# Logits of a sliding-window attention layer: 64 queries of two heads times 192 keys in place of 128 queries of one head times 256 keys

## Chip, core and metric

The kernel runs on one core of a Trainium2 chip. The metric is the time of one execution in microseconds of device time, the median of several runs. The core has five engines with queues of their own: TensorE (PE in the rows; its weight loads are listed apart as PEld), VectorE (DVE), ScalarE (ACT), GpSimd (POOL) and SyncE (SP), which here only issues DMAs.

## What is computed

The input is a sequence of 1024 tokens of width 1024. A first layer is a gated DeltaNet; after it, keys and values are computed once and shared. The second layer, which the change touches, is a sliding-window attention with 32 query heads of width 64 that share 4 key heads. Queries come in blocks of 128; a query sees itself and the 127 tokens before it, so of the 256 keys of two neighbouring blocks each query needs 128.

```python
def swa_sink_mixer(h, w_in, q_gain, sinks, w_out, k_band, v_band, bias, mask):
    q, z = jnp.split(h @ w_in, 2, axis=-1)
    q = rms_norm(q.reshape(B, T, B_Q_HEADS, B_HD), q_gain) * (B_HD ** -0.5)
    q = q.reshape(B, nb, BLOCK, B_KV_HEADS, B_GROUP, B_HD)
    logits = jnp.einsum("bnqkgd,bnskd->bnkgqs", q, k_band).astype(jnp.float32) + bias
    logits = jnp.where(mask[None, :, None, None], logits, -jnp.inf)
    sink = sinks.astype(jnp.float32).reshape(B_KV_HEADS, B_GROUP)[..., None, None]
    m = jnp.maximum(jnp.max(logits, axis=-1, keepdims=True), sink)
    p = jnp.exp(logits - m)
    probs = p / (jnp.sum(p, axis=-1, keepdims=True) + jnp.exp(sink - m))
    o = jnp.einsum("bnkgqs,bnskd->bnqkgd", probs.astype(v_band.dtype), v_band)
    o = o.reshape(B, T, B_W) * jax.nn.silu(z)
    return o @ w_out
```

## The kernel before

The heads of the second layer are worked on in 8 groups of 4 heads, each group in 8 blocks of 128 queries: 64 blocks, in the order of the list `blocks` in `b_attend`. Numbers are held as pairs of a rounded part and a rest, so a logit is the sum of two matmuls: the stationary operand is the block's queries (`qT`, which holds the rounded part of a head's queries above its rest), the moving operand the group's keys, once rounded (`kh`) and once the rest (`kl`).

The attention is one generator, `b_attend`, and the projections still to come (the next groups' queries, `b_q`, and the gate, `b_z`) are others; `interleave` draws from both by turns. TensorE's instructions stand exactly in the order in which the program is written (`manual_schedule`); the other engines' are put in order by the compiler's scheduler. Each step of the loop in `b_attend` turns the probabilities of block i, turns the queries of block i + 3, makes the logits of block i + 2 and the output of block i - 1, with matmuls of a projection between these.

In `logits`, for two heads at a time, a PSUM tile `lg` (two buffers) takes 256 columns of keys for each head: the block before, then the block itself. Since each query needs just 128 of them, VectorE folds them: where a key of the own block lies above the diagonal, `copy_predicated` (L1136) writes the logit of the previous block over it, by a mask of 128 x 128 (`self.up`). In the first block (n = 0) only the own block's 128 keys are computed and the masked ones get -1e30. Then a fused operation (L1140) adds the bias and takes the maximum with the sink, ScalarE takes the exponential (L1150), GpSimd multiplies by the reciprocal of the sum (L1154). In `turn`, TensorE transposes the folded probabilities, and the folding is undone there: the part for the own block is the transposed tile times a triangle (L1168, VectorE), that for the previous block is the rest (a copy on ScalarE, then a select on GpSimd, L1165). `values` multiplies both by the values.

The bias is loaded for each group from a table in HBM (`b_bias`, L1045), one group ahead. The sinks are loaded once in `b_consts` (L914), before the key gains `kg`. All weights come on the SP queue (L130); a weight of the second layer is scaled on GpSimd (L136) and split into a rounded part (`whi`) and a rest (`wlo`). The reciprocal root that normalises the queries (`rsqrt`, L111 to L119) is a chain of small operations on VectorE. `mm` is the PSUM tile of the projections (L939 to L941, L161 to L165), `pv` that of the output, `tp` that of the transposes.

Of the kernel before, what the change touches and what calls it, by code (L numbers as in the profile page):

```python
# [7 lines left out]
F32 = mybir.dt.float32  # L8
# [56 lines left out]
class Kernel:  # L65
# [837 lines left out]
    def b_consts(self, st):  # L903
# [190 lines left out]
    def b_attend(self, groups):  # L1094
# [15 lines left out]
        def q_turn(i):  # L1110
            t = qh.pop(i)
            ps = aps.tile([P, 4, P], F32R, name="tp", bufs=3)
            for e in range(4):
                nc.tensor.transpose(out=ps[:, e, :], in_=t[:, e, :, :].rearrange("p a d -> p (a d)"),
                                    identity=self.identr)
            qT[i] = bp.tile([P, 4, P], F32R, name="qT")
            nc.scalar.copy(out=qT[i], in_=self.f32(ps))

        def logits(i):

            X, n = blocks[i]
            kh, kl = X.keys
            sk = self.sink[:, 4 * X.hg:4 * X.hg + 4]
            q = qT.pop(i)
            k0 = 0 if n else P
            ksl = slice((n - 1) * P + k0, (n + 1) * P)
            L = Ls[i] = bp.tile([P, 4, P], F32, name="lsb", bufs=3)
            m = sb.tile([P, 4], F32, name="m")
            two = [P, 2, P]
            for pr in range(2):  # L1130
                ps = aps.tile([P, 2, 256], F32, name="lg")
                for j in range(2):
                    e = 2 * pr + j
                    nc.tensor.matmul(ps[:, j, k0:256], q[:, e, :], kh[:, ksl], start=True, stop=False)
                    nc.tensor.matmul(ps[:, j, k0:256], q[:, e, :], kl[:, ksl], start=False, stop=True)
                nc.vector.copy_predicated(ps[:, :, P:256], self.up.bitcast(I32).unsqueeze(1).broadcast_to(two),  # L1136
                                          ps[:, :, 0:P] if n else self.neg.unsqueeze(2).broadcast_to(two))
                for j in range(2):
                    e = 2 * pr + j
                    nc.vector.tensor_tensor_reduce(out=L[:, e, :], in0=ps[:, j, P:256], in1=X.bias[:, e, :],  # L1140
                                                   scale=1.0, scalar=sk[:, e:e + 1], op0=ALU.add, op1=ALU.max,
                                                   accum_out=m[:, e:e + 1])
# [3 lines left out]
            nc.vector.tensor_tensor(out=se, in0=sk, in1=m, op=ALU.subtract)  # L1146
            nc.scalar.activation(out=se, in_=se, func=AF.Exp)
# [8 lines left out]
        def turn(i):  # L1156
            L = Ls.pop(i)
            ps = aps.tile([P, 4, P], F32, name="tp", bufs=3)
            for e in range(4):
                nc.tensor.transpose(out=ps[:, e, :], in_=L[:, e, :], identity=self.ident)  # L1160
            pTs[i] = {}
            if blocks[i][1]:
                pT = pTs[i][0] = bp.tile([P, 4, P], F32, name="pT0")
                nc.scalar.copy(out=pT, in_=ps)
                nc.gpsimd.affine_select(out=pT, in_=pT, pattern=[[0, 4], [-1, P]], compare_op=ALU.is_gt, fill=0.0,  # L1165
                                        base=0, channel_multiplier=1)
            pT = pTs[i][1] = bp.tile([P, 4, P], F32, name="pT1")
            nc.vector.tensor_tensor(out=pT, in0=ps,  # L1168
                                    in1=self.cst[:, C_TRI:C_TRI + P].unsqueeze(1).broadcast_to([P, 4, P]), op=ALU.mult)

        def values(i):
            X, n = blocks[i]
            g, c = X.hg // 2, n % 4
            if c == 0:
                X.ot.append(bp.tile([P, 2, 512], F32, name="ot", bufs=4))
            po = aps.tile([P, 2, P], F32, name="pv", bufs=1)
# [6 lines left out]
            nc.scalar.copy(out=X.ot[-1][:, :, c * P:c * P + P], in_=po)  # L1183
            if n == NB - 1:
# [185 lines left out]
```

## Time and profile before

| | us |
|---|---|
| median of 3 runs | 1911.1 |
| lowest and highest run | 1909.24, 1915.82 |
| the profiled execution, its own time | 1906.83 |
| the profiled execution, span from first to last instruction | 1905.1 |

The profile is that of one execution, with start and duration of each instruction, what each engine waited for, and the granted clock of TensorE (0.994 of full speed over the span). All stretches are counted from the start of the span. The first layer, its output projection and the shared keys and values come first; the logits matmuls of the attention begin at 1174.5 us and end at 1698.4, with projections between them; from 1705 us to the end there is little but the last output projection.

### The profile page before, as it was taken

The numbers are of one execution on the slowest core, as the hardware profiler recorded it, in microseconds if no ns is written. First come the engines' busy times: TensorE is split into PE (matmuls) and PEld (weight loads), VectorE is DVE, ScalarE is ACT, GpSimd is POOL, SyncE is SP. The second block draws the span as 40 slices with busy tenths as digits, with TensorE's granted clock in tenths as the row PEclk, the third lists the DMA queues.
The fourth block names the chain that finished last, engine by engine and source line by source line (L and its number), as shares of the span: only waits on it lengthen the run. The fifth ranks groups of instructions, "written<-read, shape, count | busy, mean of one in ns | idle before, by whom it ended". The sixth has DMA issues, their size and how long they took to land.

```text
span 1905.1 us, 33635 instructions
## 1 busy us (share of the span) xinstructions
PE 1828.6 (96%) x13186; PEld 1562.9 (82%) x13186; DVE 1229.2 (65%) x2860; ACT 807.5 (42%) x1939; POOL 536.5 (28%) x554
## 2 busy tenths in 40 slices
PE   5999999999999999989999999999999999999999
PEld 4677778787877777767999998888788788879999
DVE  6767776858596776775545266777776776753432
ACT  4545353534435252433112043557756666771100
POOL 2222332323222222221311232333433343322111
PEclk9999999999999999999999999999999999999999
DMA  4511111112011211121655321111201111225542
GB/s 148 122 56 34 56 45 53 37 34 67 23 57 34 65 36 56 45 67 51 238 165 168 111 89 45 40 35 51 67 29 51 56 40 51 73 72 194 190 168 81
DMA packets 150115, 147.62 MB, mean 77 GB/s; under 512 B 7114, under 2 KB 124356, under 8 KB 149956
## 3 DMA queue, kind: packets, MB, share of 16 engines
q1 hardware_dynamic: 139616, 128.30, 21.4%
q10 hardware_dynamic: 10340, 17.16, 2.9%
q8 instruction: 104, 1.70, 0.4%
q14 instruction: 55, 0.45, 0.1%
HBM read 115.00 MB, written 30.44 MB: 76 GB/s over the span
## 4 chain that ended last, share of the span: by engine, by line
PE 36%; DVE 8%; ACT 3%; POOL 3%; issue 2%; DMA 1%; POOLq 0%; SPq 0%; ACTq 0%; DVEq 0%
PE acc L887 6%; PE acc L889 6%; PE acc L888 6%; PE mm L939 3%; PE mm L940 3%; PE mm L941 3%; PE pv L1181 2%; ACT lsb L1150 1%; PE mm L165 1%; PE mm L163 1%; PE mm L161 1%; DVE lsb L1140 1%; DVE wlo L138 1%; POOL lsb L1154 1%; PE tp L1160 1%
## 5 line engine op out<-in xcount | busy, mean ns | idle before, releaser
L161 PE MATMUL mm<-hh,whi 128*128 128x512 f32 (+1 forms) x1040 | 427.1, 411 | 1.8 <-ACT hh L223 1.7
L163 PE MATMUL mm<-hl,whi 128*128 128x512 f32 (+1 forms) x1040 | 417.5, 401 | 1.0 <-DVE hl L224 0.7
L165 PE MATMUL mm<-hh,wlo 128*128 128x512 f32 (+1 forms) x1040 | 414.8, 399 | 0.0
L138 DVE TENSOR_TENSOR wlo<-wraw,whi 128x1024 fp32r<-128x1024 f32 x141 | 178.7, 1268 | 241.0 <-POOL whi L134 216.0
L134 POOL TENSOR_SCALAR whi<-wraw 128x1024 fp32r<-128x1024 f32 x112 | 122.8, 1097 | 476.3 <-PE acc L889 241.4
L161 PEld LDWEIGHTS mm<-hh,whi 128*128 128x128 f32 x1040 | 197.0, 189 | 36.9 <-issue 5.2
L165 PEld LDWEIGHTS mm<-hh,wlo 128*128 128x128 f32 x1040 | 196.7, 189 | 36.5 <-issue 4.2
L163 PEld LDWEIGHTS mm<-hl,whi 128*128 128x128 f32 x1040 | 197.2, 190 | 34.1 <-issue 4.2
L939 PE MATMUL mm<-whi,hh 128*128 128x256 f32 x608 | 180.5, 297 | 0.0
L463 DVE SCALAR_TENSOR_TENSOR acc<-u,cw,acc 128x512 f32<-128x512 f32 x192 | 162.7, 849 | 26.5 <-POOL acc L460 24.3
L940 PE MATMUL mm<-wlo,hh 128*128 128x256 f32 x608 | 172.2, 283 | 0.0
L941 PE MATMUL mm<-whi,hl 128*128 128x256 f32 x608 | 172.2, 283 | 0.0
L887 PE MATMUL acc<-whi,hh 128*128 128x256 f32 x512 | 145.0, 283 | 0.0
L889 PE MATMUL acc<-whi,hl 128*128 128x256 f32 x512 | 144.9, 283 | 0.0
L888 PE MATMUL acc<-wlo,hh 128*128 128x256 f32 x512 | 144.9, 283 | 0.0
L1150 ACT ACTIVATE lsb<-lsb,nm 128x128 f32<-128x128 f32 x256 | 99.8, 392 | 64.1 <-DVE se L1146 54.6
L939 PEld LDWEIGHTS mm<-whi,hh 128*128 128x128 f32 x608 | 116.0, 191 | 11.0 <-issue 10.8
L940 PEld LDWEIGHTS mm<-wlo,hh 128*128 128x128 f32 x608 | 116.3, 191 | 0.2
L941 PEld LDWEIGHTS mm<-whi,hl 128*128 128x128 f32 x608 | 116.0, 191 | 0.0
L460 POOL TENSOR_SCALAR acc<-u,cw 128x512 f32<-128x512 f32 x64 | 63.9, 998 | 183.8 <-ACT u L456 169.6
L1154 POOL TENSOR_TENSOR lsb<-lsb,den 128x512 f32<-128x512 f32 x64 | 68.5, 1070 | 152.6 <-DVE den L1153 51.9
L887 PE MATMUL acc<-whi,oh 128*128 128x256 f32 x384 | 108.5, 283 | 0.0
(351 smaller groups left out, 4287.2 us busy)
## 6 DMA issues: line engine op xcount, KB each, us to landing
wraw<-in_a_w_in SPq DMA_DIRECT2D x48, 512.0 KB, 3.9
wraw<-in_a_w_out SPq DMA_DIRECT2D x32, 512.0 KB, 3.9
wraw<-in_b_w_in SPq DMA_DIRECT2D x32, 512.0 KB, 4.0
wraw<-in_b_w_out SPq DMA_DIRECT2D x32, 512.0 KB, 4.1
og<-zs SPq DMA_DIRECT2D x32, 256.0 KB, 2.0
ogT<-zs SPq DMA_DIRECT2D x28, 256.0 KB, 2.1
btab<-lt SPq DMA_DIRECT2D x1, 4096.0 KB
dm<-gd SPq DMA_DIRECT2D x8, 512.0 KB, 3.7
```

Source lines behind the costliest of these rows:

```text
L134: nc.gpsimd.tensor_scalar(out=hi, in0=raw, scalar1=1.0, scalar2=1.0, op0=ALU.mult, op1=ALU.mult)
L138: (nc.gpsimd if self.wcount < 3 else nc.vector).tensor_tensor(out=lo, in0=raw, in1=self.f32(hi), op=ALU.subtract)
L161: nc.tensor.matmul(ps, hi[:, k, :], hh[:, k, :], start=(k == 0), stop=False)
L163: nc.tensor.matmul(ps, hi[:, k, :], hl[:, k, :], start=False, stop=False)
L165: nc.tensor.matmul(ps, lo[:, k, :], hh[:, k, :], start=False, stop=(k == KT - 1))
L463: nc.vector.scalar_tensor_tensor(out=acc, in0=u[:, t:t + 512], scalar=cw[:, t, blk:blk + 1], in1=acc, op0=ALU.mult, op1=ALU.add)
L887: nc.tensor.matmul(po, oh[:, kk, ts], hi[:, kk, :], start=(k4 + kk + b == 0), stop=False)
L888: nc.tensor.matmul(po, oh[:, kk, ts], lo[:, kk, :], start=False, stop=False)
L889: nc.tensor.matmul(po, ol[:, kk, ts], hi[:, kk, :], start=False, stop=(k4 + kk + b == 7))
L939: nc.tensor.matmul(ps, hh[:, k, ts], hi[:, k % 4, :], start=(k == 0), stop=False)
L940: nc.tensor.matmul(ps, hh[:, k, ts], lo[:, k % 4, :], start=False, stop=False)
L941: nc.tensor.matmul(ps, hl[:, k, ts], hi[:, k % 4, :], start=False, stop=(k == KT - 1))
```

## The change

The 128 queries of a block are taken as two halves of 64. The halves of two heads stand together on the partitions (partition 64 e + t is query t of the half of head 2 j + e), so a stationary operand still has 128 columns. The moving operand is the 192 keys that a half can see: for the first half the previous block and the first 64 of the own, for the second the last 64 of the previous block and the own. Every query of the half sees the middle 64 of them; the first and the last 64 are seen in complementary triangles and are folded onto each other, by a mask of 64 columns (`le` for the first half, `gt` for the second). The tile index f = 2 hf + j now counts half and pair of heads in place of heads, in the logits, the probabilities, the bias, and the turned tiles; the sinks are laid out by partition halves. `turn` and `values` are rewritten to the new layout with views of runs of 64.

```diff
@@ b_consts
-        self.sink = sink = cp.tile([P, 32], F32, name="sink")
-        nc.sync.dma_start(sink, self.bcast_rows(I["b_sinks"], 32))
+        self.sink = sink = cp.tile([P, 16], F32, name="sink")
+        sk = I["b_sinks"]
+        for e in range(2):
+            nc.sync.dma_start(sink[64 * e:64 * e + 64, :],
+                              bass.AP(tensor=sk.tensor, offset=sk.offset + e, ap=[[0, 64], [2, 16], [1, 1]]))
@@ layer_b
-        self.up = self.cst[:, C_UP:C_UP + P]
+        above = self.cst[:, C_UP:C_UP + P]
+        self.gt, self.le = (bp.tile([P, 64], F32, name=i, bufs=1) for i in ("gt", "le"))
+        for r in (0, 64):
+            nc.vector.tensor_copy(self.gt[r:r + 64, :], above[r:r + 64, r:r + 64])
+        nc.vector.tensor_scalar(out=self.le, in0=self.gt, scalar1=-1.0, scalar2=1.0, op0=ALU.mult, op1=ALU.add)
@@ b_bias
-        self.nc.sync.dma_start(X.bias, bass.AP(tensor=tb.tensor, offset=tb.offset + 4 * X.hg * P * 256 + 127,
-                                               ap=[[255, P], [P * 256, 4], [1, P]]))
+        for e in range(2):
+            for hf in range(2):
+                self.nc.sync.dma_start(X.bias[64 * e:64 * e + 64, 2 * hf:2 * hf + 2, :],
+                                       bass.AP(tensor=tb.tensor,
+                                               offset=tb.offset + (4 * X.hg + e) * P * 256 + 64 * hf * 255 + 127,
+                                               ap=[[255, 64], [2 * P * 256, 2], [1, P]]))
@@ b_attend, q_turn
-            qT[i] = bp.tile([P, 4, P], F32R, name="qT")
-            nc.scalar.copy(out=qT[i], in_=self.f32(ps))
+            qT[i] = bp.tile([P, 2, 4, 64], F32R, name="qT")
+            nc.scalar.copy(out=qT[i].rearrange("p h e t -> p e h t"),
+                           in_=self.f32(ps).rearrange("p e (h t) -> p e h t", h=2))
@@ b_attend, logits
-            for pr in range(2):
+            for hf in range(2):
                 ps = aps.tile([P, 2, 256], F32, name="lg")
+                o = 64 * hf
+                cols = slice(0, 192) if n else slice(o, o + P)
+                ks = slice((n - 1) * P + o, (n - 1) * P + o + 192) if n else slice(0, P)
                 for j in range(2):
-                    e = 2 * pr + j
-                    nc.tensor.matmul(ps[:, j, k0:256], q[:, e, :], kh[:, ksl], start=True, stop=False)
-                    nc.tensor.matmul(ps[:, j, k0:256], q[:, e, :], kl[:, ksl], start=False, stop=True)
-                nc.vector.copy_predicated(ps[:, :, P:256], self.up.bitcast(I32).unsqueeze(1).broadcast_to(two),
-                                          ps[:, :, 0:P] if n else self.neg.unsqueeze(2).broadcast_to(two))
+                    w = q[:, hf, 2 * j:2 * j + 2, :].rearrange("p e t -> p (e t)")
+                    nc.tensor.matmul(ps[:, j, cols], w, kh[:, ks], start=True, stop=False)
+                    nc.tensor.matmul(ps[:, j, cols], w, kl[:, ks], start=False, stop=True)
+                if hf:
+                    nc.vector.copy_predicated(ps[:, :, P:192], gt, ps[:, :, 0:64] if n else neg)
+                elif n:
+                    nc.vector.copy_predicated(ps[:, :, 0:64], le, ps[:, :, P:192])
+                else:
+                    nc.vector.copy_predicated(ps[:, :, 0:64], gt, neg)
+                    nc.vector.memset(ps[:, :, 64:P], NEG)
...
@@ b_attend, turn
-                nc.gpsimd.affine_select(out=pT, in_=pT, pattern=[[0, 4], [-1, P]], compare_op=ALU.is_gt, fill=0.0,
-                                        base=0, channel_multiplier=1)
+                pv = pT.rearrange("p (h j) (e t) -> p h (j e) t", h=2, e=2)
+                nc.gpsimd.affine_select(out=pv, in_=pv, pattern=[[-64, 2], [0, 4], [-1, 64]], compare_op=ALU.is_gt,
+                                        fill=0.0, base=0, channel_multiplier=1)
...
@@ b_attend, values
-                    nc.tensor.matmul(po[e * 64:e * 64 + 64, :, :], v, pT[kb][:, e::2, :],
+                    nc.tensor.matmul(po[e * 64:e * 64 + 64, :, :], v, pT[kb][:, :, 64 * e:64 * e + 64],
                                      start=(kb == 1), stop=(kb == min(pT)))
```

TensorE's instructions stand in the same order as before, one for one; only the form of the logits matmuls differs. These are its rows from the last projection matmuls ahead of the second block's logits (n = 1), before:

```order
L939 MATMUL mm<-whi,hh_82 128x256
L940 MATMUL mm<-wlo,hh_82 128x256
L941 MATMUL mm<-whi,hl_83 128x256
L1134 MATMUL lg<-kh,qT 128x256
L1135 MATMUL lg<-kl,qT 128x256
```

And now:

```order
L943 MATMUL mm<-whi,hh_82 128x256
L944 MATMUL mm<-wlo,hh_82 128x256
L945 MATMUL mm<-whi,hl_83 128x256
L1151 MATMUL lg<-kh,qT 128x192
L1152 MATMUL lg<-kl,qT 128x192
```

What moved is only the shape, 192 columns for 256, and with it the line numbers.

On VectorE the scheduler sets the order anew. This is its order at the first block's logits (n = 0), where the reciprocal root of the next queries (L111 to L119, tiles `rqby` and `rqbt`) is drawn in between; before:

```order
L1136 COPY_PREDICATED lg<-cst,neg 128x2x128
L1068 TENSOR_SCALAR ssqb<-ssqb 128x16
L1107 TENSOR_TENSOR qh<-qr,qh 128x4x64
L111 TENSOR_SCALAR rqby<-ssqb 128x16
L1140 ISA lsb,m<-lg,bias,sink 128x128
L1140 ISA m 128x1
L113 TENSOR_SCALAR rqby<-rqby 128x16
L115 TENSOR_SCALAR ssqb<-ssqb 128x16
L1140 ISA lsb,m<-lg,bias,sink 128x128
L1140 ISA m 128x1
L117 TENSOR_TENSOR rqbt<-ssqb,rqby 128x16
L1136 COPY_PREDICATED lg<-cst,neg 128x2x128
```

And now:

```order
L1158 COPY_PREDICATED lg<-gt,neg 128x2x64
L1080 TENSOR_SCALAR ssqb<-ssqb 128x16
L1119 TENSOR_TENSOR qh<-qr,qh 128x4x64
L111 TENSOR_SCALAR rqby<-ssqb 128x16
L1159 MEMSET lg 128x2x64
L113 TENSOR_SCALAR rqby<-rqby 128x16
L115 TENSOR_SCALAR ssqb<-ssqb 128x16
L1162 ISA lsb,m<-lg,bias,sink 128x128
L1162 ISA m 128x1
L117 TENSOR_TENSOR rqbt<-ssqb,rqby 128x16
L1162 ISA lsb,m<-lg,bias,sink 128x128
L1162 ISA m 128x1
```

A fill (MEMSET) has come in, and the step L117 of the reciprocal root now stands between the two reductions (ISA) that read the first `lg` buffer, where it stood behind both.

## Rows read from the trace of the kernel before

**Rows 1.** Page, part 1: busy us of each engine, share of the span, instructions.
```profile
PE 1828.6 (96%) x13186; PEld 1562.9 (82%) x13186; DVE 1229.2 (65%) x2860; ACT 807.5 (42%) x1939; POOL 536.5 (28%) x554
```
**Rows 2.** Stretches: us; busy PE, PEld, DVE, ACT, POOL; granted clock; DMA share; GB/s.
```profile
1165.00:1710.00 545.00, 533.34 (x3672) 448.67 (x3671) 393.03 (x1372) 349.60 (x944) 187.29 (x211) 0.99 0.16 50
```
**Rows 3.** Waits of PE, 1165 to 1905 us: total us, times, longest.
```profile
PE tp L1160 <- POOL lsb L1154: 6.0, 4, 2.6
PE lg L1134 <- DVE m L1140: 5.0, 3, 4.2
```
**Rows 4.** Timeline of PE, a block with n = 1: start us, duration us, instruction.
```profile
1247.80 0.28 PE L1134 MATMUL lg<-kh,qT 128*128 128x256 f32 x1
1247.91 0.28 PE L1135 MATMUL lg<-kl,qT 128*128 128x256 f32 x1
...
1248.75 0.28 PE L939 MATMUL mm<-whi,hh 128*128 128x256 f32 x1
```
**Rows 5.** Timeline of PE, a block with n = 0.
```profile
1239.18 0.22 PE L1134 MATMUL lg<-kh,qT 128*128 128x128 f32 x1
1239.24 0.28 PE L1135 MATMUL lg<-kl,qT 128*128 128x128 f32 x1
1239.35 0.27 PE L1134 MATMUL lg<-kh,qT 128*128 128x128 f32 x1
1239.46 0.27 PE L1135 MATMUL lg<-kl,qT 128*128 128x128 f32 x1
...
1240.02 0.34 PE L939 MATMUL mm<-whi,hh 128*128 128x256 f32 x1
```
**Rows 6.** Timeline of PE's weight loads, the same block.
```profile
1239.19 0.19 PEld L1135 LDWEIGHTS lg<-kl,qT 128*128 128x128 f32 x1
1239.29 0.19 PEld L1134 LDWEIGHTS lg<-kh,qT 128*128 128x128 f32 x1
1239.40 0.19 PEld L1135 LDWEIGHTS lg<-kl,qT 128*128 128x128 f32 x1
```
**Rows 7.** Groups of weight loads by form: count, busy us, mean ns, idle before.
```profile
L1134 PEld LDWEIGHTS lg<-kh,qT 128*128 128x128 f32 x256 | 48.7, 190 | 8.0 <-DVE m L1140 4.4 <-issue 1.6 <-PE lg L1135 0.6
L341 PEld LDWEIGHTS mm<-hh,wab 128*32 128x32 f32 x16 | 1.7, 108 | 1.9 <-ACT u L456 0.4
```
**Rows 8.** Groups of DVE and POOL by form, 1165 to 1710 us.
```profile
L1140 DVE CUSTOM_DVE_ANT_0 lsb<-lg,bias,sink 128x128 f32<-128x128 f32 x256 | 77.9, 344 | 0.5
L1136 DVE COPY_PREDICATED lg<-cst,lg 128x256 f32<-128x256 int32 x112 | 44.6, 420 | 6.5 <-PE lg L1135 5.7
L1165 POOL TENSOR_SCALAR_AFFINE_SELECT pT<-pT 128x512 f32<-128x512 f32 x55 | 37.2, 677 | 82.2 <-ACT pT L1164 82.2
L1136 DVE COPY_PREDICATED_SCALAR lg<-cst,neg 128x256 f32 x16 | 7.6, 475 | 0.0
```
**Rows 9.** DMAs (KB each, us to landing), and issue and first use of `kg`.
```profile
abw<-in_a_w_in ACTq DMA_DIRECT2D x1, 64.0 KB, 4.2
bias<-btab SPq DMA_DIRECT2D x8, 256.0 KB, 2.9
L916 SPq DMA_DIRECT2D kg<-in_k_gain x1: 430/430/430, 17.7 to 17.7; - x1
L919 DVE SCALAR_TENSOR_TENSOR kg<-kg,lt x1: 218/218/218, 32.5 to 32.5; 128x64 f32<-128x64 f32 x1
```
**Rows 10.** Timeline of all engines at the start of the attention.
```profile
1177.57 1.90 POOL L136 TENSOR_TENSOR wraw<-wraw,gcolb 128x1024 f32<-128x1024 f32 x1 [1.09 <-DVE ssqb L115]
1177.62 1.87 DVE L117 TENSOR_TENSOR rqbt<-ssqb,rqby 128x16 f32<-128x16 f32 x1
...
1180.22 1.87 DVE L119 SCALAR_TENSOR_TENSOR rqby<-rqbt,rqby 128x16 f32<-128x16 f32 x1
...
1182.78 0.58 PE L1134 MATMUL lg<-kh,qT 128*128 128x256 f32 x1 [4.23 <-DVE m L1140]
```
**Rows 11.** Stretch with low clock, columns as in rows 2.
```profile
1180.00:1186.70 6.70, 3.92 (x19) 3.92 (x20) 6.61 (x28) 2.21 (x10) 2.31 (x2) 0.50 0.00 0
```

More of the change, by code (lines that the diff above doesn't have):

```diff
@@ L1122, in logits @@
             kh, kl = X.keys
-            sk = self.sink[:, 4 * X.hg:4 * X.hg + 4]
+            sk = self.sink[:, 2 * X.hg:2 * X.hg + 2]
             q = qT.pop(i)
-            k0 = 0 if n else P
-            ksl = slice((n - 1) * P + k0, (n + 1) * P)
             L = Ls[i] = bp.tile([P, 4, P], F32, name="lsb", bufs=3)
             m = sb.tile([P, 4], F32, name="m")
-            two = [P, 2, P]
-            for pr in range(2):
+            two = [P, 2, 64]
+            gt, le = (t.bitcast(I32).unsqueeze(1).broadcast_to(two) for t in (self.gt, self.le))
@@ L1131, in logits @@
+            neg = self.neg.unsqueeze(2).broadcast_to(two)
+            for hf in range(2):
                 ps = aps.tile([P, 2, 256], F32, name="lg")
+                o = 64 * hf
+                cols = slice(0, 192) if n else slice(o, o + P)
+                ks = slice((n - 1) * P + o, (n - 1) * P + o + 192) if n else slice(0, P)
                 for j in range(2):
-                    e = 2 * pr + j
-                    nc.tensor.matmul(ps[:, j, k0:256], q[:, e, :], kh[:, ksl], start=True, stop=False)
@@ L1140, in logits @@
-                    nc.vector.tensor_tensor_reduce(out=L[:, e, :], in0=ps[:, j, P:256], in1=X.bias[:, e, :],
-                                                   scale=1.0, scalar=sk[:, e:e + 1], op0=ALU.add, op1=ALU.max,
-                                                   accum_out=m[:, e:e + 1])
+                    f = 2 * hf + j
+                    nc.vector.tensor_tensor_reduce(out=L[:, f, :], in0=ps[:, j, o:o + P], in1=X.bias[:, f, :],
+                                                   scale=1.0, scalar=sk[:, j:j + 1], op0=ALU.add, op1=ALU.max,
+                                                   accum_out=m[:, f:f + 1])
@@ L1145, in logits @@
             se = sb.tile([P, 4], F32, name="se")
-            nc.vector.tensor_tensor(out=se, in0=sk, in1=m, op=ALU.subtract)
+            nc.vector.tensor_tensor(out=se.rearrange("p (h j) -> p h j", h=2), in0=sk.unsqueeze(1).broadcast_to([P, 2, 2]),
+                                    in1=m.rearrange("p (h j) -> p h j", h=2), op=ALU.subtract)
             nc.scalar.activation(out=se, in_=se, func=AF.Exp)
@@ L1164, in turn @@
                 nc.scalar.copy(out=pT, in_=ps)
-                nc.gpsimd.affine_select(out=pT, in_=pT, pattern=[[0, 4], [-1, P]], compare_op=ALU.is_gt, fill=0.0,
-                                        base=0, channel_multiplier=1)
+                pv = pT.rearrange("p (h j) (e t) -> p h (j e) t", h=2, e=2)
+                nc.gpsimd.affine_select(out=pv, in_=pv, pattern=[[-64, 2], [0, 4], [-1, 64]], compare_op=ALU.is_gt,
+                                        fill=0.0, base=0, channel_multiplier=1)
             pT = pTs[i][1] = bp.tile([P, 4, P], F32, name="pT1")
-            nc.vector.tensor_tensor(out=pT, in0=ps,
-                                    in1=self.cst[:, C_TRI:C_TRI + P].unsqueeze(1).broadcast_to([P, 4, P]), op=ALU.mult)
+            by = lambda t: t.rearrange("p (h j) (e t) -> p h (j e) t", h=2, e=2)
+            tri = self.cst[:, C_TRI:C_TRI + P].rearrange("p (h t) -> p h t", h=2).unsqueeze(2)
+            nc.vector.tensor_tensor(out=by(pT), in0=by(ps), in1=tri.broadcast_to([P, 2, 4, 64]), op=ALU.mult)
         def values(i):
@@ L1175, in values @@
                 X.ot.append(bp.tile([P, 2, 512], F32, name="ot", bufs=4))
-            po = aps.tile([P, 2, P], F32, name="pv", bufs=1)
+            po = aps.tile([P, 4, 64], F32, name="pv", bufs=1)
             pT = pTs.pop(i)
@@ L1180, in values @@
                 for e in range(2):
-                    nc.tensor.matmul(po[e * 64:e * 64 + 64, :, :], v, pT[kb][:, e::2, :],
+                    nc.tensor.matmul(po[e * 64:e * 64 + 64, :, :], v, pT[kb][:, :, 64 * e:64 * e + 64],
                                      start=(kb == 1), stop=(kb == min(pT)))
-            nc.scalar.copy(out=X.ot[-1][:, :, c * P:c * P + P], in_=po)
+            nc.scalar.copy(out=X.ot[-1][:, :, c * P:c * P + P].rearrange("p j (h t) -> p h j t", h=2),
+                           in_=po.rearrange("p (h j) t -> p h j t", h=2))
             if n == NB - 1:
```

1 line of the change is left out of this document (removed).

## Prediction

> **What bounds the kernel now.** I read the page's engine rows first [rows 1]: TensorE is busy 96% of the span, VectorE 65%. A busy TensorE says little by itself, since the ends of matmuls are modelled, so next come the stretch that holds the changed code and the waits in it. Between 1165 and 1710 us, the attention of the second layer with the projections laced into it, TensorE is busy 533 of 545 us, VectorE 393, ScalarE 350, GpSimd 187 [rows 2]. From there to the end two waits of TensorE make up nearly all that has a releaser, 11.0 us: 6.0 us for the normalised probabilities (lsb), 5.0 for a logits buffer in PSUM that a reduction still reads [rows 3]. So TensorE's own order, which is written by hand, sets the pace here: a nanosecond taken out of its instructions is one off the end, as long as the other engines keep up. What its instructions cost is to be read from one start to the next.
>
> **The change part by part.** *The matmuls.* There are 64 blocks (8 groups of heads by 8 query blocks) with 8 logits matmuls each. In the 8 blocks with n = 0 the moving side has 128 columns before and after. In the other 56 it goes from 256 to 192; the number of matmuls stays, and so do the 128 columns of each one's stationary side, so every weight load stays too.
>
> At 256 columns a run of eight goes from 1247.80 to 1248.75, when the next projection matmul starts: 0.95 us, 0.12 for each [rows 4]. For 192 columns the trace has no row, but a block with n = 0 bounds it from below: its eight, of 128 columns, go from 1239.18 to 1240.02, 0.84 us [rows 5]. That is surprisingly little for half the columns, and how it comes about decides the sum. The first of them is followed after only 0.06 us, and has the shortest duration, 0.22 us: its weights were already there, and 128 columns stream in 0.06 us. All later ones follow at 0.11. The weight loads beside them start 0.10 to 0.11 us apart without a break [rows 6]: from the second matmul on, the load sets the pace. A load's time goes by the stationary side's columns: 190 ns for 128, 108 for 32 [rows 7], hence (190 - 108) / 96 = 0.85 ns a column, 109 ns for 128 columns, the same 0.11.
>
> So a 192-column matmul, which by (0.12 - 0.06) / 128 = 0.46 ns a column would stream in 0.09 us, still waits for a load of 0.11. I take the 0.84 us of the 128-column run for the 192-column run: 0.95 - 0.84 = 0.11 us a block, times 56 = **6.2 us** less on TensorE. Bounds: if the stream set the pace, 0.03 us times 448 = 13.4 us; from the other side nothing, since the gap between 0.12 and 0.11 is so small that a fixed step between two matmuls could fill it.
>
> [...]
>
> *VectorE.* Masking goes from 256 to 128 elements a partition, twice a block. The 256-element form took 420 ns; the trace has none of 128. The nearest row is the reduction of 128 elements out of PSUM, 344 ns, which does more work on each, so the saving is at least 76 ns; at most it is half, 210 ns [rows 8]. I take 130, since part of 420 must be a fixed cost; 112 times 0.13 = 15 us less VectorE work in 545 us. At n = 0 one mask of 475 ns turns into a shorter mask and a fill, another into a shorter mask: about even. Three small operations make the two masks once. The reductions, exponentials and transposes keep their count and size. VectorE has 150 us of idle time in this stretch [rows 2], so I put its saving at nothing; what it could give back is part of the 11.0 us of waits.
>
> *New strides.* The copy into qT, the copy out of pv, the triangle product and GpSimd's select keep their elements, but run in pieces of 64. The select is the one whose price could move: 677 ns now [rows 8]. At twice that, 55 times 0.68 = 37 us on an engine that idles 358 us in the stretch; its result is read a block later. Cost on the path nothing; with that cover gone, up to 37 us, which I don't believe.
>
> *DMAs.* The bias of a group comes in four transfers in place of one, eight times; each landed 2.9 us after issue [rows 9], and it is asked for a whole group (545 / 8, some 68 us) ahead. SP issues three more each time, under 0.4 us each; queued behind them are weight loads and the gate's stores, fetched ahead by two weights. Nothing. The sinks come in 2048 pieces of 4 bytes in place of 128 longer ones, in the first 20 us. The nearest row is a load of 1024 pieces of 64 bytes (64 KB), which landed after 4.2 us; so 4 to 8 us in the queue. Behind them wait the key gains, asked for at 17.7 us and first read at 32.5 [rows 9]: 15 us of cover for both. Nothing; without it up to 8 us, once.
>
> *A moved order.* At the start of attention the longest wait of TensorE stands: 4.23 us before 1182.78 [rows 10]. VectorE was held up in two tiny steps of the reciprocal root, 1.87 us each, which last as long as GpSimd's scaling of a weight beside them (1.90 us). [...] In the changed order the first of these steps comes ahead of the second reduction that frees the first logits buffer, no longer behind it. That may add up to 1.9 us here, and the shorter mask takes some tenths off. I put it at nothing, with bounds of 7.6 less (wait and clock gone) and 1.9 more.
>
> The sum is -6.2 us: 1900.6 against the profiled execution's 1906.83. That one is 4.3 us below the median of the runs, 1911.1; from the median it is **1904.9 us**.
>
> **The rivals.** *The stream sets the pace* (12% likely): the load of the next weights could overlap better beneath 192 columns than beneath 128. Against it stands the unbroken row of loads [rows 6]. It gives 1911.1 - 13.4 = 1897.7. *Nothing arrives* (18%): the step from 0.12 to 0.11 belongs to something that 192 columns keep, or TensorE gains 6 us and then waits them out for probabilities, since the chain mask, reduction, exponential, product on other engines is what the 6.0 us of lsb waits come from [rows 3]. For it speaks that these waits are there at all; against it, that VectorE's part of the chain gets shorter. It gives 1910 to 1911. [...] *Slower* (10%): the moved reciprocal-root steps. [...] It decides from the point where VectorE, held up behind GpSimd's 1.9 us, is late for a reduction by more than the block of lead (8.6 us, from 1239.18 to 1247.80 [rows 4, 5]) that the written order gives it; at the start that lead does not exist yet, later it does.
>
> **How the numbers follow.** My forecast has 60%. Around its 1904.9 lie the waits, some 5 us either way. About 0.3%, 5.7 us, is what a measurement here can tell from no change, and the forecast lies just past it: of its 60 I give 33 to faster, 26 to the same, 1 to slower. With the streaming case's 12, the 18 of nothing (16 the same, 2 slower) and the 10 of slower: faster 0.45, same 0.42, slower 0.13. The range: down to the streaming case with most of the 7.6 us at the start gone as well, 1893; up to no gain and the 1.9 us more, 1913, with a little for the spread of the runs, 1914. Outside stay most of the slower case and the corner of the streaming case.
>
> **What the changed profile would show.** Right, if a run of eight 192-column logits takes 0.84 to 0.86 us, its loads 0.11 us apart; wrong, if it takes 0.70 (stream) or 0.95. The mask should show under 0.35 us, the select and the copies what they have now. TensorE's waits for lsb and for logits buffers should stay near 11 us in all, and the pause near 1182 us near 4 to 6; two or more new pauses over 2 us with a low clock behind them would make the prediction wrong. The first 60 us should not move.

## The result, and the profile after

The changed kernel takes 1953.6 us (median of 4 runs, 1948.4 to 1956.8), the kernel before beside it 1910.2 (4 runs, 1905.2 to 1915.8). The ratio is 1.0227, 95% interval 1.0204 to 1.025: slower by 43 us, where the prediction had 1904.9 and a range up to 1914.

The profiled execution's span is 1949.1 us. Page, part 1 of it, to be held against [rows 1]:

```profile
PE 1839.5 (94%) x13186; PEld 1566.6 (80%) x13186; DVE 1224.0 (63%) x2871; ACT 802.2 (41%) x1939; POOL 536.1 (28%) x554
```

All engines have about the work that they had, in 44 us more. Two stretches, columns as in [rows 2], the first from the first to the last logits matmul; and below them TensorE's waits, as in [rows 3]:

```profile
1185.00:1742.60 557.60, 520.25 (x3533) 431.14 (x3532) 375.49 (x1351) 334.17 (x922) 183.43 (x206) 0.98 0.16 48
1532.90:1538.00 5.10, 3.67 (x13) 3.08 (x14) 2.83 (x11) 2.86 (x12) 0.29 (x1) 0.72 0.01 3
```

The second row is for a pause further down. The waits of TensorE from 1165 to 1950 us:

```profile
PE tp L1183 <- POOL lsb L1177: 16.2, 16, 3.0
PE lg L1151 <- DVE m L1162: 14.6, 12, 3.7
PE lg L1151 <- DVE rqbt L117: 3.3, 3, 1.6
PE lg L1151 <- DVE rqby L119: 1.5, 1, 1.5
PE pv L1206 <- ACT ot L1208: 0.9, 3, 0.4
```

The logits run from 1185.1 to 1742.5 us, 557.4 us; in the kernel before from 1174.5 to 1698.4, 523.9 us. So 33.5 us came in this stretch, and the waits, 11.0 us before, are 36.5 in these rows. The attention also starts 10.6 us later. That part arose in the first 60 us, which "should not move". The DMA issues of the sinks, the key gains and, for comparison, the bias (count, KB each, median us to landing), as in [rows 9]:

```profile
sink<-in_b_sinks SPq DMA_DIRECT2D x2, 4.0 KB, 22.3
kg<-in_k_gain SPq DMA_DIRECT2D x1, 32.0 KB, 20.6
bias<-btab SPq DMA_DIRECT2D x32, 64.0 KB, 2.3
```

The key gains' own instructions (issue, first use):

```profile
L920 SPq DMA_DIRECT2D kg<-in_k_gain x1: 2759/2759/2759, 19.8 to 19.8; - x1
L923 DVE SCALAR_TENSOR_TENSOR kg<-kg,lt x1: 226/226/226, 40.5 to 40.5; 128x64 f32<-128x64 f32 x1
```

and the timeline of VectorE and TensorE at that place:

```profile
40.52 0.23 DVE L923 SCALAR_TENSOR_TENSOR kg<-kg,lt 128x64 f32<-128x64 f32 x1 [8.34 <-DMA lt<-in_b_q_gain]
41.46 0.58 PE L163 MATMUL mm<-hl,whi 128*128 128x256 f32 x1 [7.49 <-DVE hl L224]
```

The two loads of sinks, 4 KB each and issued 0.8 us apart, needed 22.3 us to land, the key gains behind them 20.6, and the q gains behind those, which line 923 reads as well and waited for last, 17.9. VectorE ran nothing in the 8.34 us in front of line 923, and TensorE then waited 7.49 us for the operand that VectorE had not made.

What the prediction said of single instructions held nearly: a run of logits came out at 0.87 us where it had 0.84 to 0.86, and the select, which it left as it was, takes 771 ns in place of 677. A run of eight 192-column logits, start to start, 1202.21 to 1203.08 us, as [rows 4, 5]:

```profile
1202.21 0.25 PE L1151 MATMUL lg<-kh,qT 128*128 128x192 f32 x1
1202.30 0.28 PE L1152 MATMUL lg<-kl,qT 128*128 128x192 f32 x1
1202.41 0.27 PE L1151 MATMUL lg<-kh,qT 128*128 128x192 f32 x1
...
1203.08 0.30 PE L943 MATMUL mm<-whi,hh 128*128 128x256 f32 x1
```

0.87 us: the first matmul is followed after 0.09, the others at 0.11. The median of the 56 runs is 0.871, before 0.950. The forms that answer to [rows 8], VectorE's masks and GpSimd's select:

```profile
L1156 DVE COPY_PREDICATED lg<-le,lg 128x128 f32<-128x128 int32 x56 | 16.0, 286 | 0.5 <-PE lg L1152 0.5
L1154 DVE COPY_PREDICATED lg<-gt,lg 128x128 f32<-128x128 int32 x56 | 16.3, 291 | 0.0
```

and

```profile
L1189 POOL TENSOR_SCALAR_AFFINE_SELECT pT<-pT 128x512 f32<-128x512 f32 x55 | 42.4, 771 | 84.4 <-ACT pT L1187 79.3 <-PE mm L165 5.0
```

What changed is when VectorE comes to the logits. One block behind which TensorE paused twice, in VectorE's timeline:

```profile
1527.93 2.11 DVE L1119 TENSOR_TENSOR qh<-qr,qh 128x256 fp32r<-128x256 f32 x1 [0.95 <-POOL qh L1117]
...
1531.70 0.17 DVE L117 TENSOR_TENSOR rqbt<-ssqb,rqby 128x16 f32<-128x16 f32 x1
1531.80 0.29 DVE L1156 COPY_PREDICATED lg<-le,lg 128x128 f32<-128x128 int32 x1
1531.99 0.17 DVE L118 TENSOR_TENSOR rqbt<-rqbt,rqby 128x16 f32<-128x16 f32 x1
1532.12 0.35 DVE L1162 CUSTOM_DVE_ANT_0 lsb<-lg,bias,sink 128x128 f32<-128x128 f32 x1
1532.40 0.17 DVE L119 SCALAR_TENSOR_TENSOR rqby<-rqbt,rqby 128x16 f32<-128x16 f32 x1
1532.48 0.34 DVE L1162 CUSTOM_DVE_ANT_0 lsb<-lg,bias,sink 128x128 f32<-128x128 f32 x1
1532.75 1.22 DVE L1083 TENSOR_TENSOR qr<-qr,rqby 128x1024 f32<-128x1024 f32 x1
1533.89 0.29 DVE L1154 COPY_PREDICATED lg<-gt,lg 128x128 f32<-128x128 int32 x1
1534.21 0.35 DVE L1162 CUSTOM_DVE_ANT_0 lsb<-lg,bias,sink 128x128 f32<-128x128 f32 x1
1534.49 0.35 DVE L1162 CUSTOM_DVE_ANT_0 lsb<-lg,bias,sink 128x128 f32<-128x128 f32 x1
```

TensorE, the next block's logits:

```profile
1532.98 0.33 PE L1151 MATMUL lg<-kh,qT 128*128 128x192 f32 x1 [2.42 <-DVE m L1162]
...
1534.99 0.38 PE L1151 MATMUL lg<-kh,qT 128*128 128x192 f32 x1 [1.35 <-DVE m L1162]
```

The logits of this block began at 1520.53 us. Their first mask (line 1156) ran at 1531.80, behind ten of the reciprocal root's twelve steps, whose first waited for a q operation that took 2.11 us; the second mask (line 1154) ran at 1533.89, with the scaling of q, 1.22 us, between it and the two reductions ahead. TensorE waited 2.42 us for the first buffer of the next block and 1.35 for the second, and from 1535.1 to 1538.5 us it ran at a granted clock of 0.50 (these logits matmuls start 0.21 us apart, those at 1533.2 to 1533.4 us 0.11), which makes the mean of 0.72 in the stretch from 1532.9 to 1538.0 above.

To see whether this is the rule, I took from the trace, for each of the 64 blocks, the time from its first logits matmul to the end of its last reduction. The median is 4.54 us before and 7.72 after; 3 blocks before and 17 after take over 9 us. At the one place that the prediction looked at, the start of the attention, the pause is 3.65 us where it was 4.23.

### The profile page after: what moved, and what is told of

Its sections match the earlier page's. It is cut to its first block, busy times and chain, and to the rows that moved or that the text cites. A ratio compares the mean times of both kernels' runs of the same rounds, so it can differ in the third digit from the quotient of the medians.

```text
span 1949.1 us, 33751 instructions
## 1 busy us (share of the span) xinstructions
PE 1839.5 (94%) x13186; PEld 1566.6 (80%) x13186; DVE 1224.0 (63%) x2871; ACT 802.2 (41%) x1939; POOL 536.1 (28%) x554
## 4 chain that ended last, share of the span: by engine, by line
PE 28%; DVE 12%; ACT 7%; POOL 3%; issue 2%; DMA 1%; POOLq 0%; ACTq 0%; DVEq 0%; SPq 0%
PE acc L888 6%; PE acc L887 6%; PE acc L889 6%; ACT lsb L1173 3%; DVE lsb L1162 3%; DVE wlo L138 2%; PE mm L943 1%; PE mm L945 1%; PE mm L944 1%; PE mm L163 1%; PE mm L161 1%; PE mm L165 1%; POOL lsb L1177 1%; POOL pT L1189 1%; DVE qh L1119 1%
## 5 line engine op out<-in xcount | busy, mean ns | idle before, releaser
L943 PEld LDWEIGHTS mm<-whi,hh 128*128 128x128 f32 x608 | 115.8, 190 | 11.0 <-issue 10.8
```

Of the source, the lines that this page charges most:

```text
L943: nc.tensor.matmul(ps, hh[:, k, ts], hi[:, k % 4, :], start=(k == 0), stop=False)
```

## The experiments

Two causes were to be told apart from two rivals. For the start: the small pieces of the sinks, or something that later waits cover. For the attention: the order in which VectorE's instructions stand, which the compiler chose anew; or what the change itself does, the layout in runs of 64 and the 192 columns. (Of the 2602 VectorE instructions that both kernels hold, 664 stand at another place in the row than before; of GpSimd's 550 it is 83, of ScalarE's 1496 it is 265.) All times below stand beside runs of the kernel before on the same chip, "attention" is the time from the first to the last logits matmul in the run's profile, "late" the median from a block's first logits matmul to its last reduction. The row "before" is that of the first comparison; the ratios of the others are to their own runs of before, with medians from 1906.8 to 1908.5.

| kernel | median us | ratio to before | attention us | late us |
|---|---|---|---|---|
| before | 1910.2 | 1 | 523.9 | 4.54 |
| after | 1953.6 | 1.0227 (1.0204 to 1.025) | 557.4 | 7.72 |
| e1 sinks flat | 1943.6 | 1.0166 (1.0144 to 1.0188) | 556.1 | 7.47 |
| e2 256 columns | 1913.9 | 1.0025 (1.0009 to 1.004) | 528.1 | 5.53 |
| e3 VectorE's order of before | 1915.2 | 1.0028 (1.0014 to 1.0042) | 529.8 | 4.12 |
| e4 before, VectorE's order of after | 1930.4 | 1.0104 (1.0084 to 1.0125) | 540.1 | 6.37 |
| e5 before, small pieces | 1918.9 | 1.0051 (1.0035 to 1.0066) | 524.4 | 4.55 |
| e6 three orders of before | 1903.7 | 0.9971 (0.9959 to 0.9982) | 520.3 | 4.45 |
| e7 before, three orders of after | 1953.1 | 1.0235 (1.022 to 1.025) | 566.9 | 7.80 |
| e8 before, masks earlier | 1906.0 | 0.9987 (0.9974 to 0.9999) | 519.5 | 4.34 |
| e9 as e6, 256 columns | 1904.5 | 0.9979 (0.9971 to 0.9988) | 519.4 | 4.40 |
| e10 as e6, masks earlier | 1903.0 | 0.9969 (0.9956 to 0.9982) | 516.9 | 3.80 |
| e11 as e1, 100 places ahead | 1946.9 | 1.0211 (1.0196 to 1.0227) | 562.5 | 7.54 |
| e12 as e1, short GpSimd pieces | 1938.1 | 1.0166 (1.0147 to 1.0184) | 553.2 | 6.88 |

**e1, the sinks loaded flat.**

```diff
-        for e in range(2):
-            nc.sync.dma_start(sink[64 * e:64 * e + 64, :],
-                              bass.AP(tensor=sk.tensor, offset=sk.offset + e, ap=[[0, 64], [2, 16], [1, 1]]))
+        flat = cp.tile([P, 32], F32, name="sinkflat")
+        nc.sync.dma_start(flat, self.bcast_rows(sk, 32))
...
     def layer_b(self, last):
+        for e in range(2):
+            nc.vector.tensor_copy(self.sink[64 * e:64 * e + 64, :],
+                self.sinkflat[64 * e:64 * e + 64, :].rearrange("p (c two) -> p c two", two=2)[:, :, e])
```

> The changed kernel with one thing put back: the sinks are loaded as before, one piece of 128 bytes to each partition, and two small VectorE copies at the start of the second layer sort them into the new layout; the instruction orders of all engines are as in the changed kernel. Theory (the 2048 pieces of 4 bytes hold the queue behind them, and the key gains that VectorE needs at 32.5 us come late): the first 60 us return to those of the kernel before, 8 to 10 us less than the changed kernel, about 1944 us, and the attention stays as slow as it is (some 557 us against 524). Rival (the delay is made up later, by work that waits for weights anyway): no difference.

Measured 10.0 us less by the medians. The key gains landed after 5.2 us, line 923 ran at 33.2 us, and the first logits matmul came at 1173.5, as before the change. The attention stayed at 556.1. The theory holds, and the two losses are separate.

**e5, the small pieces alone.** The kernel before, with the two loads, 2048 pieces in all, into a spare tile right behind its own.

```diff
         nc.sync.dma_start(sink, self.bcast_rows(I["b_sinks"], 32))
+        spare = cp.tile([P, 16], F32, name="spare")
+        sk = I["b_sinks"]
+        for e in range(2):
+            nc.sync.dma_start(spare[64 * e:64 * e + 64, :],
+                              bass.AP(tensor=sk.tensor, offset=sk.offset + e, ap=[[0, 64], [2, 16], [1, 1]]))
```

> The kernel before with one thing added: right behind its own load of the sinks, SyncE issues the changed kernel's two loads of them in 2048 pieces of 4 bytes as well, into a tile that nothing reads. Theory (these pieces hold the queue and so the key gains behind them): slower by 8 to 10 us, about 1918 us, all of it within the first 60 us. Rival (the delay belongs to the changed kernel's orders): within 3 us of before.

Slower by 0.51%, 9.7 us, with the same signature: the key gains land after 20.9 us. The TensorE instruction that starts at 59.9 us in the kernel before starts at 69.1 here (after: 69.3). The attention does not move, 524.4. Both directions agree.

**e2, 256 columns again.** On top of e1; the reductions' operand is moved to match.

```diff
-                cols = slice(0, 192) if n else slice(o, o + P)
-                ks = slice((n - 1) * P + o, (n - 1) * P + o + 192) if n else slice(0, P)
+                cols = slice(0, 256) if n else slice(o, o + P)
+                ks = slice((n - 1) * P, (n + 1) * P) if n else slice(0, P)
+                z = o if n else 0
...
-                    nc.vector.copy_predicated(ps[:, :, P:192], gt, ps[:, :, 0:64] if n else neg)
+                    nc.vector.copy_predicated(ps[:, :, z + P:z + 192], gt, ps[:, :, z:z + 64] if n else neg)
...
```

> As the run with the sinks loaded flat, but each logits matmul has 256 columns again, both halves of the queries times the same 256 keys; the new layout (64 queries of two heads on the partitions, masks of 64 columns, selects and copies with strides) stays. The order on VectorE comes out close to that of the kernel before. Theory (what costs is VectorE's order, in which masks and reductions of the logits stand behind the reciprocal-root steps and the scaling of q): the attention takes 520 to 530 us and the whole 1905 to 1918 us. Rival (the layout with its strides costs, the select 779 ns instead of 677 above all): it stays above 1935 us.

1913.9 us, attention 528.1: the layout with its strides is in it, and the 30 us are gone. But the compiler had chosen another order for this kernel too, so it doesn't yet say that the order was the cause.

**e3 and e4, VectorE's order exchanged.** The instructions that both kernels hold are the same in kind and number, so the order of one can be given to the other: the order of the one program as a table, and behind each instruction the next tied to it by an edge that orders the issue and waits for nothing.

```diff
...
+    for eng, text in ORDER.items():
...
+        for d in steps:
+            at += d
+            if prev is not None:
+                tc.add_manual_dep(ins[at], prev.name, info, reason="order")
+            prev = ins[at]
```

> As the run with the sinks loaded flat, with the 192 columns, and with VectorE's 2602 instructions that both kernels have held in exactly the order of the kernel before. Theory (VectorE's order is what costs): TensorE's pauses in the attention go back to some 11 us, the 4.4 us less that the narrower matmuls measured stay, and the time is 1900 to 1910 us. Rival (layout, strides, or 192 columns as such): above 1930 us.

> The kernel before, with its 256 columns, its layout and its sinks, and with nothing changed but the order of VectorE's instructions, which is exactly that of the changed kernel. Theory (the order alone costs): slower than before by 25 to 45 us, 1935 to 1955 us, with pauses of TensorE before the score transposes and the logits. Rival (the order hurts only with the new layout): within 10 us of before.

e3: 1915.2, 28 us under e1, but above the 1900 to 1910 expected. e4: 1930.4, 20 us above before by the ratio, below the 25 to 45 expected. VectorE's order is a large part, and each way something is missing. In e3's profile TensorE waits twice as long for the probabilities as before, with VectorE's order that of before:

```profile
PE tp L1186 <- POOL lsb L1180: 12.5, 6, 3.5
```

What differs there is the order of ScalarE's and GpSimd's instructions, which the compiler chose again around the pinned ones. In the same profile the first logits matmul comes at 1183.0 us (before 1174.5). This can't safely be put down to the orders: the profiled execution was the slowest of e3's ten, 1921.2 us, and ahead of the attention TensorE was busy for 22.0 us at a granted clock of 0.50, 10.1 before, which at half speed is some 6 of the 8.5 us. In e9, which has all three orders of before, it was 18.9 us, and the attention began at 1178.7.

**e6 and e7, the orders of all three engines exchanged.** The same edit with ORDER for VectorE, ScalarE and GpSimd. TensorE's order is written by hand and is the same in both kernels.

> 192 columns and the new layout, sinks loaded flat, and now ScalarE's and GpSimd's instructions too in exactly the order of the kernel before, as VectorE's. With VectorE's order alone put back the time stayed 6.7 us above before, 7.8 us of its profile lost ahead of the attention, where only ScalarE's and GpSimd's orders differed. Theory (the orders are all that costs, the narrower matmuls gain 4.4 us): ahead of the attention the time of before returns, and the whole is 1900 to 1908 us. Rival (the new layout lengthens the chain from logits to transposes, by the select's 102 ns and by twice as many short runs): the attention stays near 530 us and the whole at 1912 us or more.

> The kernel before, 256 columns and its own layout and sinks, with VectorE's, ScalarE's and GpSimd's instructions in exactly the order of the changed kernel. The run with the sinks put back, which has these orders with 192 columns and the new layout, stands 35 us above before. Theory (the orders alone cost): this one stands within 6 us of that, 1938 to 1950 us. Rival (orders and layout each bear a part): it stays at the 1930 us that VectorE's order alone gave, or below, and the rest is the layout's or the columns'.

This decides it. The changed kernel with the sinks flat and the orders of before takes 1903.7 us, 0.29% less than before, and by the ratios 11 us less than e3, which is what the orders of ScalarE and GpSimd add. The kernel before with the orders of after, its layout, columns and sinks as they were, takes 1953.1, 45 us more. That is over the 1938 to 1950 expected; the order costs it more than the changed kernel, where e1 to e6 is 37 us by the ratios. In the profiles e7's attention is 10.8 us longer than e1's: the wider logits are 4.4 of it, and TensorE was busy at a granted clock of 0.50 for 29.1 us against 16.4, some 6 us at half speed (e1's profile is of the fastest of its four runs, 1938.2 us). Against a cost of the tying itself speaks e12, which has the changed kernel's three orders tied and the ratio of e1. The same block as above, in e6:

```profile
1492.12 1.82 DVE L118 TENSOR_TENSOR rqbt<-rqbt,rqby 128x16 f32<-128x16 f32 x1
1493.86 0.28 DVE L1159 COPY_PREDICATED lg<-le,lg 128x128 f32<-128x128 int32 x1
1494.06 0.16 DVE L119 SCALAR_TENSOR_TENSOR rqby<-rqbt,rqby 128x16 f32<-128x16 f32 x1
1494.14 0.28 DVE L1157 COPY_PREDICATED lg<-gt,lg 128x128 f32<-128x128 int32 x1
1494.34 0.16 DVE L117 TENSOR_TENSOR rqbt<-ssqb,rqby 128x16 f32<-128x16 f32 x1
1494.42 0.34 DVE L1165 CUSTOM_DVE_ANT_0 lsb<-lg,bias,sink 128x128 f32<-128x128 f32 x1
...
1495.50 0.34 DVE L1165 CUSTOM_DVE_ANT_0 lsb<-lg,bias,sink 128x128 f32<-128x128 f32 x1
...
1496.24 1.23 DVE L1086 TENSOR_TENSOR qr<-qr,rqby 128x1024 f32<-128x1024 f32 x1
```

and TensorE's waits in e6, 1165 to 1950 us:

```profile
PE tp L1186 <- POOL lsb L1180: 6.3, 4, 2.0
PE lg L1154 <- DVE m L1165: 4.3, 2, 3.8
```

Here both masks stand among the steps of the reciprocal root, the four reductions follow one another with a single step between two, and the scaling of q comes behind all of them. So the last reduction ends 6.5 us after the block's first logits matmul, against 14.3 after the change, although two steps ahead of the masks took 1.75 and 1.82 us here. The next block's logits start 8.01 us after this block's (1489.35 to 1497.36), against 12.45 after the change (1520.53 to 1532.98). The waits are back at 10.6 us. In e7 they are 36.8:

```profile
PE lg L1134 <- DVE m L1140: 13.6, 11, 3.8
PE tp L1160 <- POOL lsb L1154: 12.6, 15, 2.7
PE lg L1134 <- DVE rqby L119: 6.4, 3, 3.4
PE lg L1134 <- DVE rqbt L117: 2.9, 2, 1.8
PE pv L1181 <- ACT ot L1183: 0.7, 3, 0.4
PE lg L1134 <- DVE rqby L111: 0.6, 2, 0.3
```

**e9, the layout alone.** e2's edit with e6's orders.

> The new layout, sinks loaded flat, the three orders of the kernel before, and 256 columns: beside the kernel before this changes the layout, the halved masks and the strides alone; beside the run with the three orders of before it changes 192 columns into 256 alone. Theory (the layout costs and gains nothing, the columns gain the 4.4 us): within 3 us of before, 1905 to 1911 us, 3 to 6 us above that run. Rival (the columns gain nothing and the shorter masks do): as that run, 1904 us or less.

1904.5 us, 0.21% under before: the layout with its shorter masks gains some 4 us (2.3 to 5.5 by the interval), where I had put it at nothing. Beside e6, only 0.08% higher, some 1.5 us; with intervals of 0.1% each this can't be told from nothing, and the 4.4 us that TensorE saves by the columns lie at the edge of what it leaves open. The theory missed; the rival, that the masks and not the columns gain, fits better but isn't proved. Beside e2, the same program in the compiler's own order, it is 9 us faster.

**e8 and e10, masks earlier.** e8 changes one number in the kernel before, e10 gives the resulting three orders to the changed kernel with the sinks flat.

```diff
-        self.interleave(self.b_attend(X), self.chain(back), 1.0, 20)
+        self.interleave(self.b_attend(X), self.chain(back), 1.0, 40)
```

> The kernel before with the attention's steps emitted 40 places ahead of the work that is put between them, not 20; by this VectorE's reductions of the logits stand behind fewer of the normalisation's steps (166 places fewer over 256 reductions, where the changed kernel has 205 more). Theory (places ahead of the reductions cost TensorE pauses): faster than before by 2 to 8 us, since before still lost 11 us in such waits. Rival (the normalisation that is pushed back is late for the next group's queries): slower.

> 192 columns, new layout, sinks loaded flat, and the three orders of the run in which the kernel before had the attention's steps 40 places ahead. Theory (the gains are separate and add up: 4.5 us of the columns, 2 us of the earlier masks): 1898 to 1904 us, the fastest of all. Rival (both shorten the same waits): 1903 to 1907 us.

e8 gains 2 us, with an interval that just leaves no change out; e10 at 1903.0 is the fastest here, 0.31% under before, but not to be told from e6; it lies in the theory's range and at the end of the rival's, and so decides between them nothing. Both beat the kernel before as well as the changed one. Once the pauses are rare, taking more work out of the reductions' way brings little.

**e11, a plain repair.** The same number, 20 to 100, on e1.

> The changed kernel with the sinks loaded flat and one number changed: the attention's steps are emitted 100 places ahead of the work between them, not 20, no order pinned. VectorE's reductions then stand behind 87 more other instructions than before, summed over the 256, not 205. Theory (the time goes with the places): 12 to 25 us below the run with only the sinks put back, 1919 to 1932 us. Rival (it hangs on a few places, which this does or does not mend): outside of that.

No gain but a loss: 1946.9, by the ratios 8.6 us more than e1, with intervals that do not touch, and "late" is 7.54, as after. My measure was wrong: I had counted instructions ahead of the reductions, and those that went were mostly short steps of 0.17 us. Weighted by the usual duration of their kind (1.22 us for a weight's low part, 0.68 for a triangle product, 0.2 for a short step) e11 has some 78 us more ahead of its reductions than before, the changed kernel some 100, e2 20, e8 some 30 less. That agrees with "late" better than the count did (5.53 us in e2, 4.34 in e8), but it was fitted after the result, and no run tests it. Nor does it say why e11 is slower than e1.

**e12, GpSimd's long operation cut.**

```diff
-            nc.gpsimd.tensor_tensor(out=raw, in0=raw, in1=gain.unsqueeze(2).broadcast_to([P] + shape), op=ALU.mult)
+            n, c = shape[0], shape[1]
+            cuts = [(slice(i * n // 4, i * n // 4 + n // 4), slice(0, c)) for i in range(4)]
+            parts = [nc.gpsimd.tensor_tensor(out=raw[:, r, :], in0=raw[:, r, :],
+                                             in1=gain[:, r].unsqueeze(2).broadcast_to([P, n // 4, c]), op=ALU.mult)
+                     for r, _ in cuts]
...
```

> 192 columns, new layout, sinks loaded flat, VectorE, ScalarE and GpSimd in exactly the orders of the changed kernel; GpSimd's scaling of a weight by its gain (128x1024, 1.9 us, line 136) is issued as four pieces of 128x256 one behind the other. In the changed kernel's attention 20 short VectorE steps last 0.8 us or more longer than others of their form, together 29 us over the usual, most of them steps of the reciprocal root beside this scaling; 9 of them with 12.6 us fall between the logits and the last reduction of a block. Theory (what is late are the reductions, behind whole operations of 0.7 to 1.2 us that stand ahead of them; the holds are as long in the kernel before, 21 with 31 us): within 6 us of the run with only the sinks put back, 1938 to 1948 us. Rival (the reciprocal root's steps held up behind GpSimd make the pauses, as the prediction's slower case had it): 10 us or more faster, 1934 us or less.

The pieces took 0.61 us each (median). In the attention, VectorE steps that last 0.8 us or more over the usual fell from 20 with 29.2 us to 3 with 2.5. (Between a block's first logits matmul and its last reduction, the bounds of "late", all 20 of the changed kernel lie, not the 9 named above, and all 3 of these.) The ratio is that of e1, 1.0166. So these holds are real and not what the change cost, within the 5 us or so that the two intervals leave open.

## Why the prediction was wrong

**The moved order** is the step that failed. It looked at one place, the start of the attention, and put it at "nothing, with bounds of 7.6 less and 1.9 more". There the pause in fact stayed about as it was (3.65 us for 4.23). But the order had changed through all of the attention, on three engines, and cost 45 us in the kernel before (e7) and 37 in the changed one (e1 to e6, 1.95% of 1908). With it the masks and reductions come 3 us later in the median block, and on them hang the two logits buffers in PSUM and the probabilities. The 7.6 us are the pause of 4.23 and 3.4 for the low clock, half of the 6.7 us of [rows 11], and no run shows these 3.4: the low clock began at 1180.0 us, inside the pause that lasted until 1182.78 [rows 10], and TensorE had 3.9 us of work in it. Matmuls of 256 columns start 0.21 us apart there and 0.12 outside, so by an estimate about half of the 3.9, 2.0 us, was lost beside the 4.23, 6.2 in all.

**The slower case** named the right wait and the wrong cause. It let the reciprocal root's steps, held up beside GpSimd, decide; e12 takes those holds away, and nothing that it could measure comes back. Its bound fits: TensorE idled over 0.15 us in the logits of 3 blocks before and of 11 after, and except at the start of the attention, each of these followed a block whose reductions ended later than the 8.6 us of lead, which 3 blocks exceed before and 22 after. In the block shown the next block's first matmul had to wait until 12.45 us after the logits began. "At the start that lead does not exist yet, later it does" is where it went wrong, since with whole operations of 0.7 to 1.2 us ahead of the masks the lead is used up at many places.

**The sinks** were mis-sized: "4 to 8 us in the queue", by a row of 64-byte pieces, were 22.3 us for pieces of 4 bytes, and the cover of 15 us was gone. I had named the price without cover, up to 8 us; it was 10.

**The matmuls.** The reading held: the weight loads of a run start 0.111 us apart and the matmuls 0.112 (medians; 0.119 for both before); only the first matmul, followed after 0.09 us for the 0.06 of 128 columns, showed its columns. A run takes 0.871 us, and 56 runs gain 4.4 for the 6.2 forecast. How much of it reaches the end stays open (e9).

**VectorE's saving** was sized right, 420 to 288 ns by the two forms, but "nothing" was probably too little: e9, with the new layout and the shorter masks together, has some 4 us without fewer columns.

**Strides and bias loads** were right: the select took 771 ns for 677, and e9, which has all of them, is faster than before. With the orders of before it takes 710 ns (e6, 712 in e9), so only some 34 of the 94 ns come with the strides alone.

In sum, by the ratios: 11.6 us for the sinks (1.0227 to 1.0166), 37.2 for the orders (1.0166 to 0.9971), less the 5.5 that layout and columns gain together (1 to 0.9971), 43 us. The forecast of 6.2 us less was close for the edit itself, but partly by luck: it was to come from the columns alone, and 4.0 us came without them. That 25.5 of the attention's 33.5 us are waits (36.5 less 11.0) is read from the rows; the remaining 8, and the 4.4 us that the matmuls gave, are read only in part. TensorE was busy for 16.7 us at a granted clock of 0.50 in the changed kernel's attention and for 7.4 before, at half speed 4.6 us more. An estimate gives as much again: a wait is counted from the end of the last matmul, which takes 0.28 us, while the next one otherwise starts after 0.11; so each of the 28 more waits hides 0.17 us, 4.8 in all. Some 3 us stay open. Why the compiler's orders differ so much for 64 columns less was not asked of the chip; that they do is seen in the two programs, and that e2's 256 columns bring back an order close to the old one (27 places more ahead of the reductions than before, where the changed kernel has 205).

## What to carry to other kernels

Where a compiler orders an engine, an edit of one engine's shapes can reorder the others: compare the whole orders of all engines before and after, look at what newly stands ahead of a critical operation (its number alone misled here, in e11; its duration fitted better, untested), and if the edit is good in itself, pin the old order and measure that too. Exchanging orders between two programs separates an edit from what it did to the schedule. Two loads of 4 KB in pieces of 4 bytes delayed the key and q gains queued behind them, and here the end by 9.7 us (e5, where the key gains landed after 20.9 us for 4.9); with the same numbers loaded whole and sorted by VectorE, the key gains landed after 5.2 us (e1).

## What the runs showed of the hardware

Long VectorE steps stood beside GpSimd. Two steps of the reciprocal root, at the median 0.17 us, took 1.87 us each in [rows 10], beside two scalings of a weight on GpSimd of 1.90 us; after the change a step whose form takes 0.42 us (median of 64) took 2.11 from 1527.93, beside such a scaling of 1.90 us from 1527.86. The attention has 21 VectorE steps before and 20 after that take 0.8 us or more over the median of their form, 31 and 29 us over it in all; each began while a GpSimd operation ran, 17 and 18 of them during the scaling of a weight. With that operation cut from 1.91 to 0.61 us a piece, 3 such steps are left (e12). The surprise is that some 30 us of such holds in an attention cost the end nothing that e12, with its 5 us or so of uncertainty, could measure.

Each of the sinks' two transfers, 4 KB in 1024 pieces of 4 bytes, took 22.3 us to land; issued 0.8 us apart, they were in flight together, 2048 pieces in 23 us. Neither the bytes nor the number of pieces foretells this: a load of 64 KB in 1024 pieces of 64 bytes, on another queue, landed after 4.2 us [rows 9], where half of the 23 us, an estimate, is some 11 us for 1024 pieces. Whether the difference lies in the 4 bytes, in the queue, or in all pieces reading the same few bytes of memory, no run here tells.
